# Strassen products for the second half of the first FFN's output projection, and carried-state matmuls issued side by side

## The chip, the cores and the metric

The kernel runs on one core of one Trainium2 chip. The metric is the device time of one execution in microseconds (us), the median of several runs. The core has a matrix engine (TensorE, PE in the profile, with its weight loads listed as PEld), a vector engine (VectorE, DVE), a scalar engine (ScalarE, ACT), GpSimd (POOL) and SyncE (SP), which here only issues DMAs. Each engine works off its own list of instructions in order and waits on semaphores that the other engines and the DMA queues raise.

## The reference

A trunk of two layers on 512 tokens of width 1024. Layer 0 mixes tokens by a short convolution, layer 1 by a Mamba-2 SSD (chunked state space) mixer; each is followed by a SwiGLU FFN of inner width 2816. Each of the four sub-layers is wrapped in a norm ahead and a norm behind, with shift, scale and gate from a conditioning vector `c`:

```python
mod = (silu(c) @ ada_w + ada_b).reshape(bsz, DEPTH, 2, 3, D_MODEL)
for i in range(DEPTH):
    shift, scale, gate = mod[:, i, 0]
    h = rmsnorm(x, norm_g[i, 0]) * (1 + scale) + shift
    y = short_conv_mixer(h, ...) if i == 0 else ssd_mixer(h, ...)
    x = x + gate * rmsnorm(y, norm_g[i, 1])
    shift, scale, gate = mod[:, i, 1]
    h = rmsnorm(x, norm_g[i, 2]) * (1 + scale) + shift
    g, u = split(h @ f_w_in[i], 2)
    y = (silu(g) * u) @ f_w_out[i]           # 512x2816 by 2816x1024
    x = x + gate * rmsnorm(y, norm_g[i, 3])
```

In the SSD mixer each head's output is a part within a chunk of tokens (`y_diag`) and a part from the state that earlier chunks carry over (`y_off = C · prev · exp(cs)`). All is float32.

## The kernel before

**Precision.** A float32 product is done as three matmuls in the format fp32r: each operand is split into a rounded high part (a copy on ScalarE) and the remainder (a subtraction on VectorE), and high·high, high·low and low·high go into one PSUM accumulator. Weights come from memory by DMA on SP's queue into one of two staging buffers (`wst`), and are split (`split_w`, L203 and L204; `load_w`, L221 and L222) into one of four `whl` buffers.

**Stages.** One list after the other: the modulation sums for the first norm, the convolution mixer, the first FFN (sub-layer s = 1), the SSD mixer, the second FFN. The sums of `ada_w` for the later modulations are work of VectorE (L124, one 128x512 multiply-add per eighth of the rows) that is spread over the up-projection of the first FFN: `sums(n)` issues n of them, and each second one frees a 512 KB buffer, into which SP loads the next piece (L824). Three such buffers exist.

**First FFN, up-projection.** Behind the lead (six partly finished output tiles) come 38 chunks `k` of 24 matmuls (`in_chunk`), each giving 128 columns of gate or up for all 512 tokens. ScalarE applies silu to a gate chunk, VectorE multiplies the up chunk with it, and the result is split into `ff[k]`, high and low, in one of 22 row tiles (128 of the 2816 inner columns each). The loads of the weights are written two chunks ahead, their splits one to two chunks ahead. Per four chunks 4, 4, 2 and 2 modulation sums are issued. The order on PE, SP, ACT and DVE in this part is written out by hand.

**First FFN, second product.** `out_begin` (L365) gives two generators of pieces, one for each half (512 columns) of the output, and `finish`. A piece takes four row tiles: it loads and splits their weights (`load_wo`, L233) and issues, per row tile and per token tile of 128, three matmuls 128x512 (L378 to L380) into `ys[half][token tile]`, eight PSUM accumulators. All of half 0 comes before half 1. The last two row tiles of half 0 and the last four of half 1 are left to `finish`, which runs the list `BOUNDARY` (L352): steps such as `m0_1` (the remaining matmuls of half 0, token tile 1), `sq0_1` (square and sum on ScalarE, L427), `yg0_1` (times the gate on VectorE, L431), `x0_1` (residual), `xs`, `rt3`, `rc3`, `xn` (the next norm), `tr` (transposes, L494), `u`, `hi`, `lo` (scale and shift, split, L503 to L512) and `k0_0` (first matmuls of the SSD input projection, into `li`). So the norm of the first token tiles goes on while TensorE still finishes the later ones. The six lead weights of the SSD projection (`ssd_lead`, `load_lead`, L254) are loaded in three pairs and split ahead of `BOUNDARY`. On ACT and DVE, the gates of later sub-layers (`put_gates`, L310 to L314: transpose, copy to `gr`, DMA to memory; `gr` has one buffer) were issued behind the first piece of the second product.

**Carried state in the SSD mixer.** `step_cc` (L1267 on) runs `step_c` for the two halves q of a group of heads: six matmuls `yo` (L1277, `y_off`), sixteen `yd` (L1283, `y_diag`), then on VectorE the sum of both, the skip and the gate (L1288 to L1291), and a sum of squares; for the last of the eight groups the latter ends at L1301 and feeds the matmul `ssg` (L1315).

**Second FFN.** Its second product is done by Strassen's scheme in Winograd's form. Two row tiles by two halves and 256-token blocks form a 2x2 block product with seven multiplications (`PRODUCTS`: accumulator, block of w, block of a). Its weights are prepared by `w_prep` (L1754, L1755) and its activations by `a_prep` (L1767, L1768), its block sums by VectorE (L1801) and by accumulating DMAs from POOL's queue (`w2h<-w2h`), and its matmuls are at L1789.

Of the kernel before, what the change touches and what calls it, by code (L numbers as in the profile page):

```python
# [8 lines left out]
F32 = mybir.dt.float32  # L9
# [7 lines left out]
P = 128  # L17
T = 512
# [11 lines left out]
HALVES = (slice(0, 256), slice(256, 512))  # L30
FULL = slice(0, 512)
MUL, ADD, SUB = ALU.mult, ALU.add, ALU.subtract


@with_exitstack
def trunk_kernel(
# [26 lines left out]
    def t2(name):  # L63
        return tmp.tile([P, T], F32, tag="t2", name=name, bufs=4)
# [297 lines left out]
""".split()  # L362
    LATE = 3

    def out_begin(s, w, get_act, K, gg, xn_tile, first, lead, after, stage=None):  # L365

        ys = [None, None]
        mk = (mm_ps, aux_ps) if first == "mm" else (aux_ps, mm_ps)  # L370

        def mm_tiles(hf, ks, tiles, get=get_act):
            for k, wt, kk in ks:
                a = get(k)
                for t in tiles:
                    tk = slice(t * P, (t + 1) * P)
                    pst = ys[hf][t]
                    pe.matmul(pst, a[:, 0, tk], wt[:, 0, kk, :], start=k == 0, stop=False)  # L378
                    pe.matmul(pst, a[:, 0, tk], wt[:, 1, kk, :], start=False, stop=False)  # L379
                    pe.matmul(pst, a[:, 1, tk], wt[:, 0, kk, :], start=False, stop=k == K - 1)  # L380

        def pieces(hf):
            kl = K - (2, 4)[hf]
# [16 lines left out]
        class Boundary:  # L400
# [22 lines left out]
            def sq(self, hf, t):  # L423
                st = self.st[t]
                if hf == 0:
                    st["s2"] = small(2)
                act.activation(self.junk(t, hf), ys[hf][t], AF.Square, accum_out=st["s2"][:, hf:hf + 1])  # L427

            def yg_(self, hf, t):
                self.yg[hf, t] = t2("yg")  # L430
                dve.tensor_mul(self.yg[hf, t], ys[hf][t], gg[0][:, self.cols(hf)])  # L431

            def b1(self, _, t):
                st = self.st[t]
# [99 lines left out]
                do(n, int(i))  # L534

        def finish(tail=None, ws=None):
            bd = Boundary(tail or [load_wo(w, 0, K - 2, 2), load_wo(w, 1, K - 4, 4)])
# [12 lines left out]
            return bd.h, [bd.acc[i] for i in range(6)], bd.rest, more  # L550
# [17 lines left out]
    wm_in, wm_out = m_w_in[0], m_w_out[0]  # L568

    with ExitStack() as ph:  # L570
        ada_p.append(ph.enter_context(tc.tile_pool(name="adap", bufs=3, reuse_waits="tile")))
        actp = ph.enter_context(tc.tile_pool(name="actp", bufs=22, reuse_waits="tile"))
        gx = ph.enter_context(tc.tile_pool(name="gx", bufs=1, reuse_waits="tile"))
        four = gx.tile([P, P], F32, tag="four", name="four", bufs=1)
        pool.tensor_tensor(four[:, 0:64], ident[:, 0:64], ident[:, 64:128], ADD)
        pool.tensor_tensor(four[:, 64:96], four[:, 0:32], four[:, 32:64], ADD)
# [377 lines left out]
            begun = out_finish(parts, tail, ws0)  # L954


        def ssd_lead():
            return (load_lead([(wm_in, 6144, NH), (wm_in, DIN, P)], tile4)
                    + load_lead([(wm_in, DIN + P, P), (wm_in, 2 * DIN, P)], tile4)
                    + load_lead([(wm_in, 2 * DIN + D, P), (wm_in, 0, P)], tile4))  # L960


        h, lead_ps, rest, more = begun
        acts, ws, splits, gates, lows, todo, ggs = [], list(more), [(), ()], {}, [], [], []
# [4 lines left out]
        def gate(f, pst):  # L969
            gates[f] = t2("g")  # L970
            act.activation(gates[f], pst, AF.Silu)

        def up(f, pst):
            g, a = gates[f], act_tile(f"ff{f}")
            dve.tensor_mul(g, pst, g)
            act.copy(a[:, 0, :], g)
            acts.append(a)
# [14 lines left out]
        def sums(n):  # L992
            for _ in range(n):
                have = len(fins)
                next(madds, None)
                if len(fins) > have:
                    todo.append(ada_end(have))

        with tc.manual_schedule(engines={PE_ENGINE, mybir.EngineType.SP, mybir.EngineType.Activation,
                                         mybir.EngineType.DVE}):  # L1000
# [11 lines left out]
            parts = out_begin(1, f_w_out[0], lambda k: acts[k], NF, ggs, xn_tile, "aux", ssd_lead,  # L1012
                              lambda: load_w([(wm_in, P, P)]))
            tiles = []
            for k in range(2 * NF - 6):
                if k % 2 == 0 and k < 2 * NF - 10:
                    load_pair(k // 2 + 1)
                elif k == 2 * NF - 10:
                    ops = next(parts[0])
                    splits += [(op,) for op in ops]  # L1020
# [8 lines left out]
                for op in splits[k + 2]:  # L1029
                    op()  # L1030
                low_parts()
                sums(4 if j < 2 else 2)
                if k == 2 * NF - 12:
                    ggs.append(make_gg(1, gg_tile))
            up(NF - 1, tiles[-1])
            low_parts()
            for op in ops[2:]:
                op()
            for step in todo:
                list(step)  # L1040
            next(parts[0])
# [5 lines left out]
        assert not ada_sets and not quarters  # L1047


    with ExitStack() as ph:  # L1050
        core = ExitStack()
# [98 lines left out]
        class Group:  # L1150
# [120 lines left out]
            def step_c(self, q):  # L1271

                g = self.g
                pyo = aux_ps("yo")
                for cc in range(1, NCH):
                    sl = slice(cc * P, (cc + 1) * P)
                    pe.matmul(pyo[:, sl], self.prev[:, cc - 1, q * P:(q + 1) * P], self.ct[:, sl],  # L1277
                              start=True, stop=True)
                pyd = aux_ps("yd")
                for cc in range(NCH):  # L1280
                    sl = slice(cc * P, (cc + 1) * P)
                    for hh in range(2):
                        pe.matmul(pyd[hh * HD:(hh + 1) * HD, sl],  # L1283
                                  self.xdt[:, cc, (2 * q + hh) * HD:(2 * q + hh + 1) * HD],
                                  self.e[:, 2 * q + hh, sl], start=True, stop=True)
# [3 lines left out]
                dve.scalar_tensor_tensor(y0, self.xs[q], dcol[:, 2 * g + q:2 * g + q + 1], pyd, MUL, ADD)  # L1289
                dve.tensor_add(y0[:, P:], y0[:, P:], y1[:, P:])  # L1290
                dve.tensor_mul(y0, y0, self.zs[q])  # L1291
                if q == 0:
                    self.accg = t2("accg")
                    act.activation(self.accg, y0, AF.Square)
                else:
                    sqg = t2("sqg")
                    act.activation(sqg, y0, AF.Square)
                    if g < NG - 1:
                        pool.tensor_tensor(self.accg, self.accg, sqg, ADD)
                    else:  # L1300
                        dve.tensor_add(self.accg, self.accg, sqg)  # L1301
                ygs.append(y0)
# [221 lines left out]
        with tc.manual_schedule(engines={PE_ENGINE}):  # L1524
# [10 lines left out]

    PRODUCTS = (("A", "b11", "a11"), ("B", "b21", "a12"), ("C", "b22", "a12"), ("D", "b12", "s1"),
                ("A", "b22", "a11"), ("A", "b11", "a21"), ("A", "b21", "a22"))  # L1540

    with ExitStack() as ph:
        fo = ph.enter_context(tc.tile_pool(name="fo", bufs=3, reuse_waits="tile"))
# [560 lines left out]
```

## Time and profile before

| what | value |
|---|---|
| median of 3 runs | 1341.55 us (1341.04 to 1341.75) |
| the profiled execution | 1341.48 us, span 1339.4 us, clock granted 0.999 |
| TensorE busy | 1326.9 us, 99% of the span |
| VectorE, ScalarE, GpSimd busy | 984.7, 617.9 and 65.2 us |
| up-projection's chunks of the first FFN | about 231 to 451 us |
| its second product, matmuls `y` | 451.1 to 571.2 us, 528 matmuls 128x512 |
| carried-state groups | eight, the first shown at 640.83, the last at 934.19 us |

The page gives busy time per engine, the span in forty slices, the DMA queues, the chain that ended last and the costliest groups. A group's row reads: line, engine, operation, output<-input, shape, count, then busy microseconds and the mean of one in nanoseconds, then the idle time of the engine just ahead of it and what ended it. A row of a tile gives minimum, median and maximum duration and the first and last start. A row of a timeline gives start, duration, engine, line, operation, and in brackets how long the engine had been idle before and what released it. Durations of matmuls overlap; their starts are what counts.

### The profile page before, as it was taken

How to read it: one execution, taken by the hardware profiler on the slowest of the kernel's cores; microseconds unless marked ns; L12 is line 12 of the kernel's file. 1: busy time of each engine (PE TensorE's matmuls, PEld its weight loads, DVE VectorE, ACT ScalarE, POOL GpSimd, SP SyncE). 2: the span in 40 equal slices, each digit the busy share in tenths (PEclk: the TensorE clock that was granted, in tenths of full speed). 3: DMA queues.
4: the chain of work that ended last, by engine and by line, in shares of the span. 5: the costliest groups of instructions: out<-in, count | busy, mean ns of one | idle time of the engine just before them, and what ended most of it. 6: DMA issues, size and time to landing. Idle time of an engine off the chain costs nothing.

```text
span 1339.4 us, 19134 instructions
## 1 busy us (share of the span) xinstructions
PE 1326.9 (99%) x7485; PEld 1144.0 (85%) x7485; DVE 984.7 (74%) x1581; ACT 617.9 (46%) x995; POOL 65.2 (5%) x82
## 2 busy tenths in 40 slices
PE   8999999999999999999999999999999999999997
PEld 7788889888888888898888888888789999998886
DVE  5588866778787322558889888888687777776888
ACT  5323256322222211555644555554474555554665
POOL 0000000000000000000000000000000111100320
PEclk9999999999999999999999999999999999999999
DMA  9757760677777321513543334323251888869871
GB/s 308 234 185 228 243 222 1 214 247 230 236 250 236 125 96 64 161 33 114 158 142 91 114 110 142 110 95 110 95 152 38 197 203 215 212 174 287 185 127 63
DMA packets 199887, 215.90 MB, mean 161 GB/s; under 512 B 8293, under 2 KB 148469, under 8 KB 198773
## 3 DMA queue, kind: packets, MB, share of 16 engines
q1 hardware_dynamic: 186384, 184.74, 44.5%
q0 software_dynamic: 9264, 17.04, 7.4%
q10 hardware_dynamic: 4148, 12.90, 3.1%
q8 instruction: 59, 0.97, 0.3%
q14 instruction: 32, 0.25, 0.1%
HBM read 195.37 MB, written 2.24 MB: 148 GB/s over the span
## 4 chain that ended last, share of the span: by engine, by line
PE 95%; SPq 2%; DVE 1%; ACT 1%; DMA 1%; issue 0%; DVEq 0%; ACTq 0%
PE ip L276 14%; PE ip L278 14%; PE ip L277 14%; PE sA L1694 7%; PE y L378 6%; PE y L380 6%; PE y L379 6%; PE cA L1789 4%; PE sC L1694 3%; PE li L276 3%; PE li L278 3%; PE li L277 3%; PE sB L1694 2%; PE li L756 1%; PE yd L1283 1%; PE cD L1789 1%
## 5 line engine op out<-in xcount | busy, mean ns | idle before, releaser
L276 PE MATMUL ip<-h,whl 128*128 128x512 f32 x840 | 331.3, 394 | 0.2 <-DVE cv L863 0.2
L278 PE MATMUL ip<-h,whl 128*128 128x512 f32 x840 | 327.3, 390 | 0.0
L277 PE MATMUL ip<-h,whl 128*128 128x512 f32 x840 | 327.0, 389 | 0.0
L276 PEld LDWEIGHTS ip<-h,whl 128*128 128x128 f32 x840 | 157.7, 188 | 33.7 <-issue 1.8
L278 PEld LDWEIGHTS ip<-h,whl 128*128 128x128 f32 x840 | 157.6, 188 | 33.4
L277 PEld LDWEIGHTS ip<-h,whl 128*128 128x128 f32 x840 | 157.8, 188 | 31.8
L222 DVE TENSOR_TENSOR whl<-wst,whl 128x1024 fp32r<-128x1024 f32 x99 | 120.3, 1220 | 60.3 <-ACT whl L221 60.1
L124 DVE SCALAR_TENSOR_TENSOR ada_acc<-ada_st,csil,ada_acc 128x512 f32<-128x512 f32 x140 | 104.9, 750 | 4.5 <-DMA ada_st<-in_ada_w_dram 1.1
L204 DVE TENSOR_TENSOR whlo<-wsto,whlo 128x1024 fp32r<-128x1024 f32 x41 | 49.9, 1223 | 78.5 <-ACT whlo L203 78.4
L221 ACT CAST whl<-wst 128x1024 fp32r<-128x1024 f32 x99 | 103.0, 1041 | 3.6 <-DMA wst<-in_m_w_in_dram 1.9
L276 PE MATMUL li<-h,whl 128*128 128x256 f32 x288 | 83.2, 289 | 0.0
L278 PE MATMUL li<-h,whl 128*128 128x256 f32 x288 | 81.6, 283 | 0.0
L277 PE MATMUL li<-h,whl 128*128 128x256 f32 x288 | 81.5, 283 | 0.0
L203 ACT CAST whlo<-wsto 128x1024 fp32r<-128x1024 f32 x41 | 42.6, 1049 | 76.7 <-PE y L380 75.2
L1694 PE MATMUL sA<-tq,whl 128*128 128x256 f32 x576 | 74.6, 283 | 0.3 <-DVE g L1720 0.3
L1694 PEld LDWEIGHTS sA<-tq,whl 128*128 128x128 f32 x576 | 71.6, 192 | 0.6 <-DVE g L1720 0.5
L378 PE MATMUL y<-whlo,ff 128*128 128x512 f32 x176 | 68.7, 390 | 0.0
L380 PE MATMUL y<-whlo,ff 128*128 128x512 f32 x176 | 68.5, 389 | 0.0
L379 PE MATMUL y<-whlo,ff 128*128 128x512 f32 x176 | 68.5, 389 | 0.0
L1142 DVE SCALAR_TENSOR_TENSOR cu<-ip,cols,cu 128x511 f32<-128x511 f32 (+2 forms) x84 | 62.7, 747 | 3.9 <-ACT cu L1139 1.4
L1789 PE MATMUL cA<-whlo,ao 128*128 128x512 f32 x264 | 61.2, 390 | 0.8 <-DVE ao L1768 0.4
L1789 PEld LDWEIGHTS cA<-whlo,ao 128*128 128x128 f32 x264 | 49.3, 188 | 12.2 <-ACT whlo L1754 1.2
(328 smaller groups left out, 2436.2 us busy)
## 6 DMA issues: line engine op xcount, KB each, us to landing
ada_st<-in_ada_w_dram SPq DMA_DIRECT2D x96, 512.0 KB, 5.1
wst<-in_f_w_in_dram SPq DMA_DIRECT2D x26, 1024.0 KB, 6.6
wst<-in_m_w_in_dram SPq DMA_DIRECT2D x14, 1024.0 KB, 5.3
wsto<-in_f_w_out_dram SPq DMA_DIRECT2D x10, 1024.0 KB, 5.0
wst<-in_m_w_in_dram SPq DMA_DIRECT2D x20, 512.0 KB, 5.3
wst<-in_a_w_in_dram SPq DMA_DIRECT2D x9, 1024.0 KB, 6.0
wsu<-in_f_w_in_dram SPq DMA_DIRECT2D x17, 512.0 KB, 5.7
csb<-cs_d ACTq DMA_DIRECT2D x8, 1024.0 KB, 5.5
```

The costliest lines, as they stand in the source:

```text
L124: dve.scalar_tensor_tensor(acc, w, csil[:, k:k + 1], acc, MUL, ADD)
L221: later.append((lambda sw=sw, w=w: act.copy(w[:, 0, :nk, :], sw), lambda sw=sw, w=w: dve.tensor_tensor(w[:, 1, :nk, :], sw, w[:, 0, :nk, : ...
L222: lambda sw=sw, w=w: dve.tensor_tensor(w[:, 1, :nk, :], sw, w[:, 0, :nk, :].bitcast(F32), SUB)))
L276: pe.matmul(dst, w_at(w, 0, kk), a[:, 0, sl], start=start, stop=False)
L277: pe.matmul(dst, w_at(w, 0, kk), a[:, 1, sl], start=False, stop=False)
L278: pe.matmul(dst, w_at(w, 1, kk), a[:, 0, sl], start=False, stop=stop)
L378: pe.matmul(pst, a[:, 0, tk], wt[:, 0, kk, :], start=k == 0, stop=False)
L379: pe.matmul(pst, a[:, 0, tk], wt[:, 1, kk, :], start=False, stop=False)
L380: pe.matmul(pst, a[:, 1, tk], wt[:, 0, kk, :], start=False, stop=k == K - 1)
L1142: dve.scalar_tensor_tensor(u[:, sft:], pst[:, :T - sft], w[3 - sft], u[:, sft:], MUL, ADD)
L1694: pe.matmul(dst, w[:, wl, k0 + k, :], moving(q, k, al), skip_group_check=True, start=q in ("P1", "P5", "P2") and k == 0 and i == 0, stop=k ...
L1789: pe.matmul(bank[r][sub], a[:, al, q, tk], w[:, hl, q, :], start=first and k == 0, stop=last and k == 2, skip_group_check=True)
```

## The change

1. Of the 22 row tiles of the first FFN's inner width, the first 16 (`NS`) go through the seven products of halves: 8 pairs of row tiles, each a 2x2 block problem (rows 2p and 2p+1 by the two halves of the output, and two 256-token blocks). An item is one of the seven products for two neighbouring pairs: 28 items of 12 matmuls 128x512. The rest of the row tiles (16 to 21) is multiplied as before into the same eight accumulators, partly between the items, partly in `BOUNDARY`. The order of items `seq` is 28 Strassen items with four plain ones set among them, 32 in all (q = 0 to 31).
2. The gated activations of the 16 tiles stay in float32 (`raw`), and VectorE forms their block sums in place. The weights are loaded whole (`x_load` in chunks 16, 20 and 24 of the up-projection, `xy_load` in the last, `y_load` behind the last) and combined by accumulating DMAs on POOL's queue (24 of 256 KB) and by VectorE (8).
3. An accumulator takes the sum of several products that more than one block of the output needs. `behind` therefore keeps intermediate sums in six tiles (`held`: C11 and C12 and C22 for two token tiles each, 128x512), and in `BOUNDARY` VectorE adds each to its accumulator in front of the square (`sq`); the square and the gate then read that sum.
4. `put_gates(2)` and `(3)` and the preparation of items 2 and 3 stand between the last chunk and the first product. The tail's weights (row tiles 18 to 21 of half 1, 20 and 21 of half 0) and the SSD lead weights are loaded from item 27 on, in space that `raw` and the weights held.
5. The modulation sums go 4, 4, 3, 3 per four chunks. Pools are placed anew. POOL is in the hand-written order.
6. In `step_cc` both runs of `yo` come before both `yd`.

```diff
+        tiles_s = [[(i, p), (i, p + 1)] for i in range(7) for p in range(0, n_s, 2)]
+        seq = [("s", n) for n in range(len(tiles_s))]
+        seq[6 * per:6 * per] = [("p", 1, NS, (2, 3), 1)]
+        seq[5 * per:5 * per] = [("p", 1, NS, (0, 1), 0)]
+        seq += [("p", 0, NS, range(4), 2), ("p", 0, NS + 2, range(4), 3)]
...
+        def w_prep(item):
+            w = w_of[item] = whl_p.tile([P, 2, 2, T], F32R, tag="whl", name="whlo")
...
+            for sl, src in todo_w:
+                act.copy(w[:, 0, sl, :], src)
+                dve.tensor_tensor(w[:, 1, sl, :], src, w[:, 0, sl, :].bitcast(F32), SUB)
...
+        def product(item):
+            for sub in range(2):
+                for q, (i, p) in enumerate(tiles_s[item[1]]):
...
+                    w, a, tk = w_of[item], a_of[item], slice(sub * P, (sub + 1) * P)
+                    for k, (wl, al) in enumerate(((0, 0), (1, 0), (0, 1))):
+                        pe.matmul(bank[r, sub], a[:, al, q, tk], w[:, wl, q, :], start=first and k == 0,
+                                  stop=False, skip_group_check=True)
...
+        def behind(q):
+            for t in range(2):
+                if q == at["s", per - 1]:
+                    held[0, t] = t2("c11")
+                    act.copy(held[0, t], bank["A", t])
+                elif q == at["s", 4 * per - 1]:
+                    held[1, t] = t2("c12")
+                    act.copy(held[1, t], bank["D", t])
+                elif q == at["s", 5 * per - 1]:
+                    dve.tensor_tensor(held[1, t], held[1, t], bank["A", t], SUB)
+                elif q == at["s", 6 * per - 1]:
+                    held[1, 2 + t] = c22[:, t, :]
+                    act.activation(c22[:, t, :], bank["A", t], AF.Copy, scale=-1.0)
+            for p in range(n_s):
+                if q == 5 + p // 2:
+                    add_(b_("b22", p), b_("b12", p))
+                if q == 12 + p:
+                    add_(b_("b21", p), b_("b22", p))
+                if q == 9 + p:
+                    dve.tensor_tensor(b_("b11", p), b_("b22", p), b_("b11", p), SUB)
...
             for q in (2, 3):
                 list(put_gates(q, mm_ps))
-        begun = out_finish(parts)
+            for p in range(n_s - 2):
+                y_load(p)
+            for p in range(n_s):
+                add_(b_("b12", p), b_("b11", p))
+            w_prep(seq[2])
+            w_prep(seq[3])
+            a_prep(seq[2])
...
+                if q + 4 < len(seq):
+                    w_prep(seq[q + 4])
+                if q + 3 < len(seq):
+                    a_prep(seq[q + 3])
+                if q == 27:
+                    st_p.close()
...
+                    for xn, (hf, k0) in zip(xns, tails):
+                        plain[hf, k0] = plain_load(hf, k0, xn)
+                    for load in ssd_lead[:2]:
+                        leads += load(lead_ops)
...
+                    for op in lead_ops[3 * (q - 28):3 * (q - 27)]:
+                        op()
+                    if q == 29:
+                        leads += ssd_lead[2](lead_ops)
...
             def sq(self, hf, t):
...
-                act.activation(self.junk(t, hf), ys[hf][t], AF.Square, accum_out=st["s2"][:, hf:hf + 1])
+                src = ys[hf][t]
+                if (hf, t) in held:
+                    src = self.yg[hf, t] = held[hf, t]
+                    dve.tensor_add(src, ys[hf][t], src)
+                act.activation(self.junk(t, hf), src, AF.Square, accum_out=st["s2"][:, hf:hf + 1])
...
             def step_cc(self):
-                self.step_c(0)
-                self.step_c(1)
+                off = [self.step_o(q) for q in range(2)]
+                for q in range(2):
+                    self.step_c(q, off[q])
```

More of the change, by code (lines that the diff above doesn't have):

```diff
@@ L363, in trunk_kernel, with out_begin @@
     LATE = 3
-    def out_begin(s, w, get_act, K, gg, xn_tile, first, lead, after, stage=None):
-        ys = [None, None]
+    def out_begin(s, w, get_act, K, gg, xn_tile, first, lead, after, stage=None, ys=None, held=None):
+        ys = [None, None] if ys is None else ys
+        held = {} if held is None else held
         mk = (mm_ps, aux_ps) if first == "mm" else (aux_ps, mm_ps)
@@ L377, in mm_tiles @@
                     pst = ys[hf][t]
[L378 to L380 removed]
+                    for i, (al, wl) in enumerate(((0, 0), (0, 1), (1, 0))):
+                        pe.matmul(pst, a[:, al, tk], wt[:, wl, kk, :], start=k == 0 and i == 0,
+                                  stop=k == K - 1 and i == 2, skip_group_check=bool(held))
         def pieces(hf):
@@ L536, in finish @@
         def finish(tail=None, ws=None):
+            if tail == ():
+                return mm_tiles
             bd = Boundary(tail or [load_wo(w, 0, K - 2, 2), load_wo(w, 1, K - 4, 4)])
@@ new lines, in xy_load, with b_ @@
+        def xy_load(p):
+            w4[p] = wst_p.tile([P, 4, T], F32, tag="wst", name="w2s")
+            for c in range(2):
+                dma(w4[p][:, 2 * c:2 * c + 2, :], w_rows(p, c))
+        def b_(name, p):
+            r, c = int(name[1]) - 1, int(name[2]) - 1
+            if p in w4:
+                return w4[p][:, 2 * c + r, :]
+            return wy[p][:, r, :] if c else wx[p // 2][:, p % 2, r, :]
+        tiles_s = [[(i, p), (i, p + 1)] for i in range(7) for p in range(0, n_s, 2)]
@@ L1045, in trunk_kernel @@
+            for op in lead_ops[12:]:
+                op()
+            begun = finish(tail_w, leads)
         h, lead_ps, rest, wz1 = begun
-        assert not ada_sets and not quarters
     with ExitStack() as ph:
```

176 lines of the change are left out of this document (147 added, 29 removed).

## The prediction

> **What bounds the kernel now.** I read the page first (busy time, the forty slices, the chain that ended last), then the lines by shape, the tile of the second product, the chain and the timelines at the two ends of the stage.
>
> ```profile
> span 1339.4 us, 19134 instructions
> PE 1326.9 (99%) x7485; PEld 1144.0 (85%) x7485; DVE 984.7 (74%) x1581; ACT 617.9 (46%) x995; POOL 65.2 (5%) x82
> PEclk9999999999999999999999999999999999999999
> PE 95%; SPq 2%; DVE 1%; ACT 1%; DMA 1%; issue 0%; DVEq 0%; ACTq 0%
> ```
>
> TensorE is busy for 99% of the span and carries 95% of the chain that ended last, at full clock. So removed matmul time is removed time, as long as nothing else then makes TensorE wait. The rows of the second product, and of the second layer's FFN, where the same seven-product scheme runs already:
>
> ```profile
> L378 PE MATMUL y<-whlo,ff x176: 389/389/476, 451.1 to 570.7; 128*128 128x512 f32 x176
> L380 PE MATMUL y<-whlo,ff x176: 388/389/393, 451.5 to 571.2; 128*128 128x512 f32 x176
> 1226.59 14.28 PE cA L1789 x63
> L1789 PE MATMUL cA<-whlo,ao 128*128 128x512 f32 x264 | 61.2, 390 | 0.8 <-DVE ao L1768 0.4
> ```
>
> Three lines of 176 are 528 matmuls. Each lasts 0.389 us, but they overlap: 63 of the same size take 14.28 us in the chain, 0.2267 us each. That pitch, not the duration, is the price of one. I call E = 451.1 the start of the product. The windows:
>
> ```profile
> core 0: us, PE busy (x) PEld busy (x) DVE busy (x) ACT busy (x) POOL busy (x), PEclk, DMA share, GB/s
> 30.00:35.00 5.00, 4.77 (x78) 3.58 (x77) 1.27 (x6) 1.56 (x3) 0.00 (x0) 1.00 1.10 350
> 290.00:320.00 30.00, 30.00 (x135) 24.84 (x134) 22.99 (x34) 7.78 (x10) 0.00 (x0) 1.00 0.80 255
> 451.00:555.00 104.00, 104.00 (x461) 86.01 (x461) 30.71 (x32) 25.08 (x28) 0.00 (x0) 1.00 0.36 112
> 555.00:572.00 17.00, 17.00 (x82) 14.11 (x81) 12.04 (x28) 13.72 (x36) 0.00 (x0) 1.00 0.44 127
> ```
>
> The up-projection (290 to 320) has VectorE at 77% and DMA at a share of 0.80; the product has both idle for two thirds. The change fills the second and adds some to the first.
>
> **The change part by part.**
>
> *Matmuls.* 16 row tiles by seven products: 28 items of 12 matmuls, 336. Six row tiles left: 6 × 24 = 144. Together 480 for 528: 48 × 0.2267 = −10.9 us.
>
> *Steady part of the product.* An item lasts 12 × 0.2267 = 2.72 us. Its work on the other engines goes by these rows of the second FFN:
>
> ```profile
> L1755 DVE TENSOR_TENSOR whlo<-w2t,whlo 128x1024 fp32r<-128x1024 f32 x12 | 14.7, 1222 | 5.5 <-ACT whlo L1754 5.5
> L1768 DVE TENSOR_TENSOR ao<-raw,ao 128x512 fp32r<-128x512 f32 x25 | 17.1, 683 | 0.0
> L1801 DVE TENSOR_TENSOR w2t<-w2t 128x512 f32<-128x512 f32 x5 | 3.4, 683 | 0.0
> w2h<-w2h POOLq DMA_DIRECT2D x12, 256.0 KB, 4.4
> ```
>
> VectorE per item: low part of the weights 1.22, of the activations 0.68, at most one addition 0.68: 2.58, and some 0.07 less per operation because they overlap, about 2.4 of 2.72. ScalarE has 1.05 + 0.58. Both prepare three or four items ahead, so I cost it at nothing; the cover is gone where VectorE passes 2.72, and each 0.1 over would cost 28 × 0.1 = 2.8. The 24 accumulating DMAs on POOL's queue (empty from 451 to 555) land in 4.4 us by the row; the nearest reader of one stands four items, 10.9 us, behind its issue: nothing.
>
> [...] The 4.4 us row was taken beside the low parts and additions quoted with it, and TensorE's idle there is 0.8 us in the L1789 row, so this trace does not bear out a delay that matters, and the sum goes by the row.
>
> *Up-projection.* Four chunks take 4 × 5.44 = 21.8 us (24 matmuls each). The modulation sums go at 14 per four chunks for 12, seven loads of 0.524 MB for six; with 2.1 MB of weights and one of three 1.05 MB loads of w_out that is 6.8 MB, 313 GB/s. VectorE gets 2 × 0.75 us more on 21.8: 77% to 84%. Between 255 and 350 GB/s in the rows; nothing if the queue runs at the 350, since sums have three buffers. I take nothing and price the other end as a rival.
>
> *Entry.* Behind the last chunk VectorE now takes both gate pieces (put_gates of 2 and 3) before it prepares the third item; in the kernel before they lay under four rows of matmuls:
>
> ```profile
> 462.24 0.28 DVE L313 COPY gr<-ggp 8x128 f32<-8x128 f32 x1 [3.19 <-PE ggp L310]
> 464.41 0.27 DVE L313 COPY gr<-ggp 8x128 f32<-8x128 f32 x1
> 462.55 0.30 SPq L314 DMA_DIRECT2D gate_d<-gr  x1
> 464.98 0.36 SPq L314 DMA_DIRECT2D gate_d<-gr  x1
> ```
>
> gr has one buffer: the second copy waits until the first's DMA on SP has landed, 462.55 to 464.41, at most 1.86. From E: the last up-projection tile's product, rounding and low part to +2.3 (three 128x512 operations in a row, 0.7 to 0.8 each), first copy +2.5, its DMA +4.4, second copy +4.7. Behind it stand item 2's low part and two activation steps (1.2 + 0.7 + 0.7, less overlap: to +7.3) and the last subtraction: +7.7. Two items of 12 (5.4), the gate's few transposes and the third item's first two matmuls keep TensorE until about +6.1. Stall 1.6 (0.9 where the DMA lands in half the time, 2.2 where a semaphore's delay adds). SP waits on the second copy too, and six loads of 512 KB stand behind it; these feed item 8 (+21.8), landing by about +17.6: nothing.
>
> *Exit.* B = 569.61 − 66 × 0.2267 = 554.65 is where the hand-over to the next norm begins on TensorE; its order is the same.
>
> ```profile
> 547.99 4.80 SPq L254 DMA_DIRECT2D wst<-in_m_w_in_dram  x4
> 552.19 1.14 ACT L203 CAST whl<-wst 128x512 fp32r<-128x512 f32 x2 [1.68 <-DMA wst<-in_m_w_in_dram]
> 557.66 1.15 ACT L203 CAST whl<-wst 128x512 fp32r<-128x512 f32 x2 [0.54 <-DMA wst<-in_m_w_in_dram]
> 558.71 0.59 ACT L427 ACTIVATE xn<-y 128x512 f32<-128x512 f32 x1
> 567.19 1.32 ACT L485 ACTIVATE xn<-x,ss 128x512 f32<-128x512 f32 x2
> 569.61 0.60 PE L494 MATMUL xtr<-ident,xn 128*128 128x128 f32 x4
> 571.28 0.43 DVE L512 TENSOR_TENSOR h<-u,h 128x256 fp32r<-128x256 f32 x1 [1.48 <-ACT h L508]
> 571.78 0.36 PE L276 MATMUL li<-h,whl 128*128 128x256 f32 x1
> ```
>
> Before, the last lead weights' casts let the first square start at B + 4.1 (558.71); from it to the end of the normalised rows (568.5) are 9.8 us; the transposes at 569.61 have 1.1 us in hand. After, two things are later. First, the tail's weights and the lead weights land in space that the Strassen operands held. The preparation of item 31 waits for the weight slot of item 27, which ends 12 + 12 + 24 + 24 matmuls before B, at B − 16.3; cast 1.05 and subtraction 1.22 with their hand-overs: B − 13.75, and only then SP issues the first tail load, two more tails, four lead loads. The third lead pair waits for a staging slot that VectorE frees with the fourth lead operation, about B − 1; by the row of 547.99 a load of this kind is cast 4.2 us after issue (552.19), its second half 1.65 later, and then two casts and subtractions follow. The first square comes at B + 6.7 to 8.15, with the first held addition ahead of it. Second, four of the six held additions (128x512 from PSUM, 0.69 each) lie in the chain to the normalised rows: 9.8 + 2.85 = 12.65. Together B + 19.4 to 20.8, for a place on TensorE at B + 15.0: a stall of 4.4 to 5.8, of which I take 4.8, and 0.2 more at the first lead matmul, which had 0.07 in hand (571.71 to 571.78). So +5.0. Bounds: 2, if the lead loads land under the last items and only the additions count (2.85 less the 1.1 in hand); 7, if the third pair waits for the last tail as well.
>
> *Carried-state matmuls.* In eight SSD groups the two yo runs now stand side by side:
>
> ```profile
> 640.83 0.83 PE L1277 MATMUL yo<-ct,prev 128*128 128x128 f32 x6
> 641.59 1.09 PE L1283 MATMUL yd<-csb,xdt 128*64 128x128 f32 x16
> 642.62 0.94 PE L1277 MATMUL yo<-ct,prev 128*128 128x128 f32 x6
> 643.48 1.09 PE L1283 MATMUL yd<-csb,xdt 128*64 128x128 f32 x16
> 936.12 0.73 DVE L1289 SCALAR_TENSOR_TENSOR yg<-xs,dcol,yd 128x512 f32<-128x512 f32 x1
> 942.32 0.69 DVE L1301 TENSOR_TENSOR accg<-accg,sqg 128x512 f32<-128x512 f32 x1 [0.70 <-ACT sqg L1297]
> 943.44 1.02 PE L1315 MATMUL ssg<-accg,ones 128*128 128x512 f32 x2
> ```
>
> The second yo run after a yd run takes 0.86 to the next start, the first, after full-width matmuls, 0.76. Two switches between widths become one: about 0.2 a group (0.1 to 0.35), −1.6 (0 to −2.8). But the first yd, and VectorE behind it, comes about 0.8 later; in the last group VectorE starts at 936.12 right behind it, and its end (943.01) is 0.43 ahead of TensorE at 943.44: 0.6 later costs about 0.5 once. Net −1.1 (−2.8 to +0.5).
>
> *Sum.* −10.9 + 1.6 + 5.0 − 1.1 = −5.4, against the profiled run's own 1341.48 (span 1339.4 and 2.1 around it; the median, 1341.55, is 0.07 away): 1336.1 us.
>
> **The rivals.**
>
> *The clock falls at the exit.* The start of the kernel shows it at half speed:
>
> ```profile
> 2.50 4.41 PE L671 MATMUL xtr<-ident 128*128 128x128 f32 x20
> 15.73 1.28 PE L671 MATMUL li<-ident 128*128 128x128 f32 x10
> PE ptr L93 <- DMA rows<-in_c_dram: 2.3, 1, 2.3
> ```
>
> The same transposes take 0.22 us at the start and 0.13 later. If five idle microseconds bring that state back, 4.4 us run at half rate, +2.2: 1338.3. The trace before cannot tell: its longest wait of TensorE is 2.3, and the forecast stall is twice that. [...]
>
> *The exit is hidden.* Loads land early and the additions fit into the gaps of VectorE: 1341.5 − 10.9 − 1.1 + 1.6 = 1331.1. For it: VectorE has 12.04 us of work in 555 to 572. Against it: the chain above is serial, and only 1.1 us were in hand.
>
> *The up-projection starves: slower than before.* If the queue gives only the 255 GB/s of its window, 1.27 MB are missing in each 21.8 us from chunk 16 to 28: 3.8 MB, 15 us late. A weight load has about 8 us in hand (landing three before its cast, and a chunk of 5.4 until TensorE needs it). So TensorE waits 7 us or more, with no gain to pay for it but the 5.4: 1343, and up to 1351 where the loads have nothing in hand. It decides from a lag of 13.4. Against it: 350 GB/s at 30 to 35.
>
> **How the numbers follow.** What can be told from no change is about 0.2%, 2.7 us: faster is below 1338.8, slower above 1344.2. Likeliest (both stalls as worked out): 0.46, 1336.1, its own range 1333 to 1339. Clock: 0.19, 1338.3, half of it below 1338.8. Hidden: 0.17, 1331.1. Starved: 0.13, of which 0.1 is above 1344.2. Left: 0.05 for a loss in a place I do not see. Faster 0.44 + 0.10 + 0.17 = 0.71; slower 0.10 + 0.04 = 0.14; same 0.15. From 1331 to 1342 leaves out about half of the hidden case's lower side and nearly all of the starved one: 2 in 10.
>
> **What would show it.** Right: 480 matmuls at 0.2267 us between the last chunk and the boundary's end; one gap of 1 to 2 us in TensorE six microseconds behind the last chunk, put down to VectorE; one of 4 to 6 at the first transposes, put down to the normalised rows; a yo run of 12 in eight groups. Wrong: gaps inside the items (VectorE as the bound, or POOL's adds late), a gap in the up-projection between chunks 16 and 30, matmuls of 0.42 us spacing behind the exit, or no gap at the exit at all.

## The result, and the profile after

The changed kernel takes 1337.86 us (median of 8 runs, 1336.63 to 1339.06), the kernel before, on the same chips, 1341.65 us (1341.04 to 1342.06). The ratio is 0.9973, with a 95% interval of 0.9962 to 0.9984: 3.8 us faster, a little over what can be told from no change. The profiled execution took 1338.20 us, its span 1336.4 us.

From the page of the changed kernel, the busy time; below it, the three waits of TensorE that matter here (what it waited for: microseconds in all, times, the longest):

```profile
PE 1316.8 (99%) x7437; PEld 1136.7 (85%) x7437; DVE 1028.1 (77%) x1654; ACT 641.9 (48%) x1042; POOL 85.9 (6%) x106
```
```profile
PE xtr L502 <- ACT xn L493: 6.0, 1, 6.0
PE cA L1127 <- DVE ao L1108: 0.8, 1, 0.8
PE cC L381 <- DVE whlo L207: 0.4, 1, 0.4
```

The 48 matmuls are gone (7485 to 7437), but there are three waits in the first FFN that were not there, one of 6 us at the first transposes (xtr). The windows around it:

```profile
core 0: us, PE busy (x) PEld busy (x) DVE busy (x) ACT busy (x) POOL busy (x), PEclk, DMA share, GB/s
470.00:530.00 60.00, 60.00 (x266) 49.71 (x265) 46.99 (x67) 36.13 (x58) 16.75 (x20) 1.00 0.62 118
560.00:570.00 10.00, 3.81 (x11) 2.76 (x11) 7.16 (x18) 8.36 (x25) 0.00 (x0) 0.73 0.00 1
570.00:575.00 5.00, 5.00 (x38) 4.94 (x37) 3.84 (x9) 2.35 (x8) 0.00 (x0) 0.86 0.00 0
```

Inside the product (470 to 530) TensorE is full and VectorE 78% busy. At the end of the wait and behind it the granted clock (PEclk) is 0.73 and 0.86, where the kernel before has 1.00. Ten times 0.27 and five times 0.14 make 3.4 us of clock lost: at half clock (PEclk reads 0.50 from 564.75 to 571.25) that is 6.8 us. TensorE's rows show it (`li` are the lead matmuls of the SSD projection); the last line is the third lead matmul of the kernel before:

```profile
558.62 1.52 PE L381 MATMUL cD<-whlo,ff 128*128 128x512 f32 x6
566.19 1.51 PE L502 MATMUL xtr<-ident,xn 128*128 128x128 f32 x4 [6.05 <-ACT xn L493]
567.36 2.91 PE L381 MATMUL cD<-whlo,ff 128*128 128x512 f32 x6
...
571.34 0.32 PE L281 MATMUL li<-h,whl 128*128 128x256 f32 x1
```
```profile
572.10 0.29 PE L278 MATMUL li<-h,whl 128*128 128x256 f32 x1
```

Six matmuls 128x512 take 1.52 us ahead of the wait and 2.91 behind it, four transposes 1.51 for 0.60 before the change. From the first transposes to the third lead matmul it is 5.15 us (566.19 to 571.34), before the change 2.49 (569.61 to 572.10). Where the time came from is read best between landmarks of the two traces, since both executions begin a little differently: the first `ip`, the first `yo` of the SSD mixer, the last `ip`. Of the kernel before (first two lines) and the changed one (last two), first and last start at the end of each line:

```profile
L276 PE MATMUL ip<-h,whl x840: 388/389/578, 60.8 to 1225.8; 128*128 128x512 f32 x168
L1277 PE MATMUL yo<-ct,prev x96: 270/275/377, 640.8 to 936.6; 128*128 128x128 f32 x96
```
```profile
L279 PE MATMUL ip<-h,whl x840: 389/389/578, 60.4 to 1222.3; 128*128 128x512 f32 x168
L1485 PE MATMUL yo<-ct,prev x96: 270/275/275, 640.1 to 932.3; 128*128 128x128 f32 x96
```

From the first `ip` to the first `yo`, which holds all of the Strassen part: 580.0 before, 579.7 after. From the first `yo` to the last `ip`, which holds the eight carried-state groups: 585.0 before, 582.2 after. So in these two executions the Strassen part gave 0.3 us and the regrouping 2.8; how far one execution can be trusted for this is seen below.

### The profile page after: what moved, and what is told of

It reads as the page before. It is cut to its first block, busy times and chain, and to the rows that moved or that the text cites. A ratio compares the mean times of both kernels' runs of the same rounds, so it can differ in the third digit from the quotient of the medians.

```text
span 1336.4 us, 19228 instructions
## 1 busy us (share of the span) xinstructions
PE 1316.8 (99%) x7437; PEld 1136.7 (85%) x7437; DVE 1028.1 (77%) x1654; ACT 641.9 (48%) x1042; POOL 85.9 (6%) x106
## 4 chain that ended last, share of the span: by engine, by line
PE 93%; DVE 2%; DMA 2%; ACT 1%; issue 1%; SPq 0%; DVEq 0%; ACTq 0%
PE ip L279 14%; PE ip L281 14%; PE ip L280 14%; PE y L381 10%; PE sA L1904 7%; PE cA L1999 4%; PE sC L1904 3%; PE li L279 3%; PE li L280 3%; PE li L281 3%; PE cA L1127 2%; PE li L767 2%; PE sB L1904 2%; PE yd L1496 1%; PE cD L1999 1%; PE cC L1999 1%
## 5 line engine op out<-in xcount | busy, mean ns | idle before, releaser
L381 PE MATMUL y<-whlo,ys 128*128 128x512 f32 x384 | 89.4, 392 | 0.0
L381 PEld LDWEIGHTS y<-whlo,ys 128*128 128x128 f32 x384 | 71.7, 188 | 15.9 <-issue 0.7
L1860 DVE TENSOR_TENSOR whl<-wsu,whl 128x1024 fp32r<-128x1024 f32 x33 | 40.4, 1223 | 23.4 <-ACT whl L1859 23.4
L279 PEld LDWEIGHTS li<-h,whl 128*128 128x128 f32 x288 | 55.4, 192 | 0.0
L280 PEld LDWEIGHTS li<-h,whl 128*128 128x128 f32 x288 | 55.3, 192 | 0.0
```

What stands on the lines that cost most here:

```text
L279: pe.matmul(dst, w_at(w, 0, kk), a[:, 0, sl], start=start, stop=False)
L280: pe.matmul(dst, w_at(w, 0, kk), a[:, 1, sl], start=False, stop=False)
L381: pe.matmul(pst, a[:, al, tk], wt[:, wl, kk, :], start=k == 0 and i == 0, stop=k == K - 1 and i == 2, skip_group_check=bool(held))
L1860: dve.tensor_tensor(dst[:, 1], src, dst[:, 0].bitcast(F32), SUB)
```

## The experiments

### The two parts alone

The kernel before with the regrouping, and the changed kernel without it:

```diff
 # on the kernel before
             def step_cc(self):
-                self.step_c(0)
-                self.step_c(1)
+                off = [self.step_o(q) for q in range(2)]
+                for q in range(2):
+                    self.step_c(q, off[q])
```

> The kernel before with only the two yo runs of a group side by side. Theory (the landmarks of the two traces: from the first yo to ssg the changed kernel gains 2.5 us more, while up to the first yo it has gained only 0.7): 2.3 to 2.9 us faster than before, about 1339.0. Rival (the prediction's net term): 1.1 us, about 1340.5.

> The changed kernel with yo and yd in the old order. Theory: the 48 matmuls that are saved are given back almost whole in the first FFN, so it stands 0.2 to 1.2 us below the kernel before, about 1340.7. Rival (the Strassen part carries the gain, as in the prediction): 4.3 us below, about 1337.3.

Measured: the regrouping alone 1338.81 us (11 runs; before 1341.58; ratio 0.9981, 0.9972 to 0.9990), 2.8 us faster. The Strassen part alone 1340.85 us (11 runs; ratio 0.9995, 0.9987 to 1.0004), 0.7 us below, which its interval does not tell from no change. The two add up to 3.5 of the 3.8. So the first theory holds by the medians: the part with 10.9 us of matmul time in it is worth less than 1 us (its interval allows 1.7), and the small one carries the gain.

The trace of the Strassen part alone has 578.3 us from the first `ip` to the first `yo`, 1.7 less than before and 1.4 less than the changed kernel, whose code is the same there. Its exit wait is 5.9 us, the short wait at `cC` is missing, and of its 6.8 us at half clock 4.0 fall on work instead of 5.2: the clock fell 3.1 us into the wait instead of 4.4. So single traces of this stretch scatter by more than 1 us.

The rows of the changed kernel for one group of heads and for the last; below them, the end of the first group in the kernel before:

```profile
640.07 1.50 PE L1485 MATMUL yo<-ct,prev 128*128 128x128 f32 x12
641.50 1.97 PE L1496 MATMUL yd<-csb,xdt 128*64 128x128 f32 x32
643.40 0.50 PE L279 MATMUL ip<-h,whl 128*128 128x512 f32 x1
...
931.07 1.50 PE L1485 MATMUL yo<-ct,prev 128*128 128x128 f32 x12
...
940.17 1.10 PE L1528 MATMUL ssg<-accg,ones 128*128 128x512 f32 x2
```
```profile
644.51 0.50 PE L276 MATMUL ip<-h,whl 128*128 128x512 f32 x1
```

A group goes from 640.07 to 643.40, 3.33 us, where it took 3.68 (640.83 to 644.51): 0.35 saved, 2.8 in eight. The `yo` give 0.19 of it (1.43 for 0.76 and 0.86), the `yd` 0.16 (1.90 for twice 1.03). In the last group `ssg` follows 9.10 us behind the first `yo`, before 9.25: the later VectorE work there cost at most 0.2.

### The clock behind the wait

```diff
 # BOUNDARY: one step ahead of the first transposes
-... xn1_1 xn0_1 sq1_2 tr0_0 ...
+... xn1_1 xn0_1 sq1_2 fl0_0 tr0_0 ...
+        def none_of(n):                      # fl0_0, n = 20; none[0] is a tile of zeros
+            for _ in range(n):
+                pe.matmul(ys[1][3], none[0][:, :P], none[1][:, 0, 0, :], start=False, stop=False, ...)
```

> The changed kernel with 20 matmuls 128x512 by a tile of zeros (4.5 us) set on TensorE ahead of the first transposes, in the time in which it would wait; they add nothing to the accumulator they go to. Theory (6 us without work drop TensorE's clock, which costs 2.7 us behind the wait): the wait shrinks to about 1.5 us, the transposes start at the same time, the clock stays at 1.00 and the time falls by 2.4 to 3, to about 1335.1. Rival (the matmuls behind the wait are slow because their operands come late): no gain, 1337.9 or more.

Measured: 1336.20 us (5 runs, 1335.66 to 1337.87; ratio 0.9965, 0.9953 to 0.9978). TensorE's rows of this kernel:

```profile
560.14 4.70 PE L552 MATMUL cD<-whlo,gap 128*128 128x512 f32 x20
566.31 0.33 PE L504 MATMUL xtr<-ident,xn 128*128 128x128 f32 x1 [1.48 <-ACT xn L495]
...
567.22 1.64 PE L383 MATMUL cD<-whlo,ff 128*128 128x512 f32 x6
...
569.37 0.28 PE L281 MATMUL li<-h,whl 128*128 128x256 f32 x1
```

The transposes start when they did (566.31 for 566.19), the six matmuls behind them run at full pitch (1.64 us for 2.91), and the third lead matmul starts at 569.37 for 571.34. From the first `ip` to the first `yo` it takes 577.1 us, 2.6 less than the changed kernel, as expected; 2.1 of it lie between the first transposes and the third lead matmul (3.06 us for 5.15), the rest ahead of them. The median fell by only 1.7, and the two intervals overlap, so the size rests on one trace of each. That work on TensorE in the wait kept the clock up is shown directly: PEclk is 1.00 in every window from 545 to 580.

Whether such a wait drops the clock without any Strassen product was asked of the kernel before, with VectorE delayed ahead of the same transposes:

```diff
 # on the kernel before, n = 6 and n = 11; xn[3][1] is overwritten later
             def rc3(self, _, t):
+                if (s, t) == (1, 1):
+                    for _ in range(n):
+                        dve.tensor_mul(self.xn[3][1], gg[0][:, self.cols(0)], gg[0][:, self.cols(0)])
```

> The kernel before with six extra multiplications on VectorE (3.7 us, their result is not used) ahead of the last reciprocal before the first transposes of the same boundary. Theory (a wait of about 2.6 us does not drop the clock): TensorE waits 2.6 us, clock 1.00 behind it, time 2.6 above the kernel before, 1344.2. Rival (any wait of this size drops it): 1345.5 or more, half-speed rows behind the wait.

> The same with eleven multiplications (6.7 us). [...] Rival (the slow rows of the changed kernel belong to its Strassen part and not to the wait): 5.6 above, 1347.2, clock 1.00.

Measured: 1344.90 us with six (ratio 1.0024, 1.0015 to 1.0033), 1350.35 with eleven (1.0065, 1.0051 to 1.0078). TensorE's rows with six, then with eleven:

```profile
572.32 0.90 PE L497 MATMUL xtr<-ident,xn 128*128 128x128 f32 x3 [2.58 <-ACT xn L488]
...
573.45 0.63 PE L379 MATMUL y<-whlo,ff 128*128 128x512 f32 x1
```
```profile
575.50 0.90 PE L497 MATMUL xtr<-ident,xn 128*128 128x128 f32 x3 [6.05 <-ACT xn L488]
...
576.63 0.63 PE L379 MATMUL y<-whlo,ff 128*128 128x512 f32 x1
```

A wait of 6.05 us costs 8.7 (1350.35 against 1341.62), so 2.7 beyond itself, also without Strassen: this rival falls. With 2.58 us the trace has half-speed rows too (0.63 us each, starts 0.43 apart). But the ten runs of that kernel fall into two groups: five take 1344.00 to 1344.61 us at a granted clock of 0.999, five 1345.20 to 1346.04 at 0.997 or 0.998, and the profiled one (1345.70) is of the second. The first group stands 2.7 above the kernel before, the wait alone, as the expectation had it; the second stands 4.0 above. So after this wait the clock seems to have fallen in half of the runs (only one has a trace): there the rival came true, in the others the expectation, and the median of 1344.90 lies between.

### What makes the transposes late

The chain of the changed kernel, the stretch that ends at the first held addition (start, duration, what):

```profile
528.21 1.06 ACT whlo L206
529.30 1.24 DVE whlo L207
530.55 0.37 SPq L1083
...
532.04 0.41 SPq L257
532.50 9.43 DMA wst<-in_m_w_in_dram
...
544.75 0.69 DVE whl L207
545.46 0.37 SPq L257
545.88 5.45 DMA wst<-in_m_w_in_dram
551.35 0.63 ACT whl L206
552.00 1.29 DVE whl L207 x2
553.30 0.61 DVE c L432
```

Item 31's split at 528.21 holds back the tail's loads (530.55) and the lead loads (532.04); the third lead pair is issued at 545.46, when VectorE frees its staging slot, lands by 551.35, and only when it is split comes the first held addition (`c`, 553.30). Two edits tell the loads from the additions. The first moves the third pair's four splits into the boundary:

```diff
-... yg0_0 m1b_0 ... rt1_0 yg1_0 m1a_1 ... k0_1 rc1_2 ... k0_2 x1_2 ...
+... yg0_0 ld0_0 m1b_0 ... rt1_0 yg1_0 ld2_0 m1a_1 ... k0_1 ld1_0 rc1_2 ... k0_2 ld3_0 x1_2 ...
-                    for op in lead_ops[3 * (q - 28):3 * (q - 27)]:
+                    for op in lead_ops[3 * (q - 28):min(8, 3 * (q - 27))]:
```

The second exchanges the two token blocks, so that the held sums fall mostly on the last two token tiles:

```diff
-            return v[:, :, int(name[2]) - 1, HALVES[int(name[1]) - 1]]
+            return v[:, :, int(name[2]) - 1, HALVES[2 - int(name[1])]]
-                        hf, t = {"B": (0, 0), "A": (0, 2), "C": (1, 0), "D": (1, 2)}[r]
+                        hf, t = {"B": (0, 2), "A": (0, 0), "C": (1, 2), "D": (1, 0)}[r]
```

> The changed kernel with the third pair of lead weights split inside the boundary (four splits placed behind yg0_0, yg1_0, k0_1 and k0_2) and no longer ahead of the first held addition. Theory (the chain to the first transposes starts late because ACT and DVE wait there for that pair's load): the first held addition starts about 4 us earlier, the wait at the transposes falls from 6.0 to some 2 to 3 us, too short to drop the clock, and the time falls by 5 to 7, to about 1332. Rival (the held additions and the chain itself hold the transposes): the chain starts earlier but the two early splits in it take the gain back; less than 2 us faster, 1336 or more.

> The changed kernel with the two 256-token blocks exchanged in the seven products, so that of the first two token tiles only the second half of the output has a held sum (two additions in the chain to the first transposes instead of four, the first square needs none). Theory (held additions are a part of the exit wait, the late third lead pair another): the first square comes 1.3 us earlier, the chain is 0.6 to 1.2 shorter, the wait falls from 6.0 to about 4; the clock still drops for a part; 2 to 3.5 us faster than the changed kernel, about 1335.2. Rival (the additions lie in gaps of VectorE): less than 0.7 us, 1337.3 or more.

Measured: late splits 1337.22 us (6 runs; ratio 0.9970, 0.9958 to 0.9981), exchange 1337.85 us (5 runs, 1335.94 to 1337.98; 0.9969, 0.9957 to 0.9981). By the medians neither gained what its theory said. The waits at the transposes, of the first and of the second:

```profile
PE xtr L502 <- ACT xn L493: 4.8, 3, 4.0
```
```profile
PE xtr L502 <- ACT xn L493: 4.7, 1, 4.7
```

With late splits the first held addition came 4.3 us earlier (548.89 for 553.22 in VectorE's timeline), but the longest wait shrank by only 2.0, to 4.0, and the clock still fell in that trace (PEclk 0.83 from 560 to 570). That 2 to 3 us would be too short for a fall was an estimate of mine, which this run did not come to test. VectorE's rows of that kernel show what took the rest:

```profile
551.10 0.68 DVE L207 TENSOR_TENSOR whl<-wst,whl 128x512 fp32r<-128x512 f32 x1
...
555.29 0.69 DVE L207 TENSOR_TENSOR whl<-wst,whl 128x512 fp32r<-128x512 f32 x1 [1.43 <-ACT whl L206]
```

Two splits stand inside the chain, one behind an activation table load of 1.28 us on ScalarE (at 553.16). So the time is the rival's (1336 or more), and its reason is seen: the late pair had started the chain late, as the theory said, and my placing put it back in. The exchange shortened the wait by 1.35 us in its trace, but its median is the rival's too; the profiled run (1335.94) was 1.9 us below its other four, and I cannot say why.

### All three, and then with nothing in the chain

The next kernel has the exchange, the third pair's casts and subtractions singly at other places, and the gate pieces behind items 1 and 4:

```diff
-            for q in (2, 3):
-                list(put_gates(q, mm_ps))
...
+                if q in (1, 4):
+                    list(put_gates(2 + q // 4, mm_ps))
...
-... rt1_0 yg1_0 m1a_1 sq0_1 rc1_0 x0_0 m1b_1 ...
+... rt1_0 la0_0 yg1_0 lb0_0 m1a_1 sq0_1 la2_0 rc1_0 x0_0 lb2_0 m1b_1 ...     # la: cast on ACT, lb: subtraction on DVE
```

> Token blocks exchanged, the third lead pair's casts and subtractions set singly into gaps of the boundary, and the two gate pieces moved from the entry behind items 1 and 4. Theory (the giving back of the saved matmuls is the exit chain, the clock behind it and the gate's DMA at the entry): the first square starts near 547, the normalised rows end before TensorE's place at about 560, no wait over 1 us at either end, clock 1.00 throughout; 8 to 9.5 us faster than the changed kernel, 1328.4 to 1330. Rival (something else, such as the loads of the lead weights, takes the place of the removed wait): a wait of 2 us or more remains, 1332 or more.

Measured: 1334.71 us (5 runs; ratio 0.9949, 0.9936 to 0.9963). TensorE's rows:

```profile
562.18 0.33 PE L505 MATMUL xtr<-ident,xn 128*128 128x128 f32 x1 [3.01 <-ACT xn L496]
...
563.09 2.21 PE L384 MATMUL cC<-whlo,ff 128*128 128x512 f32 x6
```

The entry wait was gone from the list of waits. At the exit 3.0 us stayed, with the clock down in part (2.21 us for six). So the rival holds, with a wait over 2 us and a time over 1332. The splits in the chain were the suspect, so they went behind the transposes, and the held addition of another token tile into a gap:

```diff
-... rt1_0 la0_0 yg1_0 lb0_0 m1a_1 sq0_1 la2_0 rc1_0 x0_0 lb2_0 m1b_1 ... b3_0 rt1_1 yg1_1 ... hi0_0 sq0_3 tr0_1 lo0_0 u0_2 ...
+... rt1_0 yg1_0 m1a_1 sq0_1 rc1_0 x0_0 m1b_1 ... b3_0 rt1_1 ad0_2 yg1_1 ... hi0_0 la0_0 la2_0 sq0_3 tr0_1 lo0_0 lb0_0 lb2_0 u0_2 ...
```

> As the kernel with all three edits, but the third lead pair's first two splits stand behind the first transposes (ACT behind hi0_0, VectorE behind lo0_0), and the held addition of half 0, token tile 2, stands in the gap of VectorE ahead of yg1_1. In the kernel with all three, the chain from the first held addition to the normalised rows was 14.15 us against 13.53 in the changed kernel, with two splits and one held addition of another token tile inside it and a table load that VectorE waited for. Theory (these took the place of the removed wait): the chain is 11.5 to 12, the rows end near 560.3, the wait falls from 3.0 to under 1 us, which does not drop the clock; 2.5 to 4.5 us faster than that kernel (1334.7), about 1331.2. Rival (the chain is held by ACT's own work, which is the same): a wait of 2 us or more stays, and less than 1 us is gained.

The last kernel is this one without the exchange of the blocks (and without `ad0_2`):

> The fastest kernel so far (1332.0) without the exchange of the token blocks: the third lead pair's splits stay behind the transposes and the gates behind items 1 and 4, but four held additions lie in the chain again and the first square waits for one. Theory (each held addition in the chain is wait on TensorE, once the late weights are out of the way): the first square near 549.7 for 546.6, the chain 13 us from the first addition, rows end near 562.5, wait 2.2 to 2.8, clock partly lost; 2.5 to 4.5 us slower than with the exchange, about 1335.5. Rival (additions lie in gaps of VectorE): within 1 us of 1332.

Measured: 1332.04 us with the exchange (5 runs, 1331.12 to 1332.22; ratio 0.9927, 0.9913 to 0.9940), 1333.13 without it (5 runs, 1332.28 to 1333.64; 0.9936, 0.9923 to 0.9950). TensorE's rows at the transposes, with and without:

```profile
559.89 0.33 PE L506 MATMUL xtr<-ident,xn 128*128 128x128 f32 x1 [0.23 <-ACT xn L497]
...
560.81 1.62 PE L384 MATMUL cC<-whlo,ff 128*128 128x512 f32 x6
...
576.23 0.33 PE L506 MATMUL xtr<-ident,xn 128*128 128x128 f32 x1 [1.05 <-ACT xn L497]
```
```profile
560.95 0.33 PE L505 MATMUL xtr<-ident,xn 128*128 128x128 f32 x1 [1.74 <-ACT xn L496]
561.57 0.55 PE L505 MATMUL xtr<-ident,xn 128*128 128x128 f32 x3 [0.28 <-ACT xn L496]
561.87 1.64 PE L384 MATMUL cD<-whlo,ff 128*128 128x512 f32 x6
```

Without splits in the chain the wait at the first transposes is 0.2 us, the clock stays up (PEclk 1.00 in every window from 545 to 580), and the kernel is 9.4 us faster than the one before and 5.8 faster than the changed one. A wait of 1.05 us now stands at later transposes (576.23), behind the place to which the splits moved; that they cause it was not tested. Without the exchange the first wait is 1.7, the clock stays up in the trace (1.00 in the same windows), and the median is 1.1 us higher: nearer to the rival than to the theory. The intervals of the two kernels overlap, though no run of the one is as slow as the fastest of the other. So the larger part of what was lost, 4.7 us of exit, clock and entry together, hung on the places of the third lead pair and of the gate pieces, and about 1 us on the held additions.

## Why the prediction was right, and where it was not

The forecast was 1336.1 us, 1331 to 1342, and faster with 0.71; 1337.86 lies inside, 1.8 above the point. Which terms would matter, and through which waits, was right. That the point came so near is in part luck: the exit with the clock cost 3.7 us more than forecast, and the regrouping, which gave 1.7 more, and the entry, which cost 0.4 less, took more than half of that back. Of the cases set out, it was the clock's (1338.3, chance 0.19) that came true and not the likeliest: its sign, half-speed matmuls behind the exit, is in the rows.

- *Matmuls, −10.9.* Right. The count fell by 48. The fastest kernel shows that most of the time can be had: it stands 6.8 us below the regrouping alone (1332.04 against 1338.81), of which 10.9 would be all. Of the 4.1 that are missing its trace lists 2.1 us as waits of TensorE from the product's tail to the transposes at 576.84; the rest stays open.
- *Steady part, nothing.* Right: no wait inside the items, VectorE 78% busy for the 88% worked out. POOL's additions landed in 4.2 to 5.9 us, beside 4.4 in the row of the second FFN, and no wait of TensorE is put down to them. VectorE's operations beside them are all TENSOR_TENSOR (88 between 455 and 530).

```profile
w2y<-w2x POOLq DMA_DIRECT2D x6, 256.0 KB, 5.9
w2s<-w2s POOLq DMA_DIRECT2D x6, 256.0 KB, 4.2
```

- *Up-projection, nothing.* Right: from the first `ip` to the first `cA` at 450.63 it takes 390.2 us, as from the first `ip` to `y` before (390.3). The starved rival did not come.
- *Entry, +1.6 (0.9 to 2.2).* Right in place, too large: 0.8, just below its range. The chain has the gate's DMA with 1.2 us, where I had taken 1.86, and the second copy starts 0.1 behind its landing (454.32 for 454.20); the longer delay that made the upper end of the range was not seen:

```profile
452.98 1.22 DMA gate_d<-gr
```

  0.4 more at 547.83, where TensorE waited for a tail weight's split, was not in the sum.
- *Exit, +5.0 (2 to 7).* Right in mechanism and chain, and mis-sized for want of the clock. Nearly each step stands in the chain above: the tail load forecast for B − 13.75 came at B − 14.5 (B, 66 matmuls ahead of TensorE's place for the transposes at 560.0, is 545.0 here), the third pair's issue forecast for about B − 1 at B + 0.5, the first square for B + 6.7 to 8.15 at B + 9.0 (553.99, right behind the first addition), and the chain of 12.65 took 12.8. (The 2.85 for four additions is 0.71 each, where the row quoted has 0.69; it makes no difference.) The wait was 6.05 for 4.8. And the clock's fall, which I held as a rival with 0.19 and priced at 2.2, came on top of it: 5.2 us of work ran at half clock, 2.6 more. Likeliest case and rival were not alternatives, as I set them: a wait this long brought the fall on. The price was taken from slow rows at the start of the kernel, where PEclk reads 1.00; whether these are the same thing is not shown.
- *Carried state, −1.1 (−2.8 to +0.5).* Mis-sized too. I took 0.2 a group, which is what the `yo` gave (0.19); the `yd`, which I had left out, gave 0.16 more, and 0.35 is the upper end of my bound. I charged 0.5 for the last group, which cost at most 0.2. So −2.8.

With the measured sizes: −10.9 + 0.8 + 0.4 + 6.05 + 2.6 − 2.8 = −3.85. One thing is still missing in it: a wait is listed from the end of the matmul before, 0.389 us behind its start, while a matmul is priced at its pitch of 0.2267, so each of the three waits costs 0.16 more than its row. With these 0.5 it is −3.35; the two profiled executions differ by 3.3 (1338.20 against 1341.48), the medians by 3.8. For the Strassen part alone the sum makes −0.55, beside −0.3 between the landmarks of these two traces, −1.7 in its own trace, and −0.7 and −0.95 by the medians (against the kernel before, and against the regrouping alone): within the scatter. The hidden rival's 1331.1 is what the last two kernels come near to, but not by its sum, which kept 1.6 for the entry and took 1.1 for the regrouping; with everything hidden it would be 1341.5 − 10.9 − 2.8 = 1327.8.

## What to carry to other kernels

Matmul time that a new scheme saves can be lost at its two ends, as some 10 of 10.9 us were here: look for what the new stage makes late (here a staging slot and the loads behind it), and for every operation in the in-order chain to the next stage's first instruction. A wait of TensorE of 1.74 us was harmless here in its trace, one of 2.58 by their times not in half of the runs, and those of 3.0 to 6.05 not in theirs: count the clock's fall with a wait of that length, and put independent work into the wait (20 matmuls kept PEclk at 1.00) or take operations out of the chain. Measure each part of a change alone: by the medians the small edit that came along was worth some three times the large one.

## What the hardware showed beyond this

The clock fell after a shorter wait than expected (2.58 us), and not in every run. In the traces no wait at the boundary's transposes up to 1.74 us (with 0.28 more behind it) was followed by slow rows; 2.58, 3.0, 4.0, 4.7, 5.9 and 6.05 us all were, at about half the rate (0.43 us between starts for 0.2267). What PEclk lost over the windows gives the time at half clock, and only two lengths occur in these seven traces: 3.4 us (waits of 2.58, 3.0 and 4.0) and 6.8 (4.7, 5.9 and both of 6.05). In windows of a quarter of a microsecond the fall begins 2.1 us (exchange) to 4.4 us (changed kernel) after TensorE's last matmul ends; in the kernel with all three edits it begins 1.7 us after work has come back. So the same wait costs more or less by where the fall lies: 5.2 us of slowed work in the changed kernel, 4.0 in the Strassen part alone, and, by their times, none in five of the ten runs with 2.58 us.
